# Rotating a 8192 x 8192 float32 matrix on one core: the first block of loads and the last one divided by rows

## The chip, the cores and the metric

The kernel runs on one core of one Trainium2 chip. The metric is device time in microseconds (us) of that core, from start to end of one execution; lower is better. The median of 19 runs stands for the kernel before.

## The reference

```
def setup_inputs():
    return {"x": np.random.randn(8192, 8192).astype(np.float32), "k": 1}

def reference(x, k):
    return np.rot90(x, k)
```

With k = 1 this is a quarter turn: `out[i, j] = x[j, 8191 - i]`, a transpose with the order of columns reversed. No arithmetic is done on the values. 268.44 MB have to be read and 268.44 MB written.

## The kernel before

The matrix is taken in 16 macro tiles: 8 bands of 1024 rows (`R`), and in each band two blocks of 4096 columns (`C`). A macro tile passes through these steps.

- Load (L82, issued by SP, the sync engine). Eight row tiles of 128 rows x 4096 columns, 2 MB each, one DMA per row tile, into a pool of two buffers (`a_pool`).
- Reverse (L89, VectorE). Each row tile is copied in eight chunks of 512 columns. The copy reverses the order inside each group of 128 columns. The chunks are kept in a pool of 68 buffers (`r_pool`); a macro tile needs 64 of them.
- Transpose (L104, TensorE). For each group of 128 columns the eight row tiles are transposed, 128 x 128 at a time, against an identity matrix, into PSUM. A PSUM tile holds 2048 values per partition, that is two groups of columns x 1024 rows, and needs 16 transposes. There are two PSUM tiles.
- Evict (L109, ScalarE). Each PSUM tile is copied to half of an output buffer. There are two output buffers (`o_pool`), each of 2 MB: four groups of columns x 1024 rows.
- Store (L115, issued by ScalarE's own queue). When two copies have filled a buffer, it is stored as one DMA of 2 MB: in each of the 128 partitions four pieces of 1024 values, 4 KB each, go to four rows of the output that lie 128 rows apart.

So a macro tile has eight loads and eight stores, all of 2 MB. No store of a macro tile can be made before its last load has landed, because each store needs all its row tiles.

`whole_reads` changes the source side of the stores alone: the four pieces of a partition, which lie side by side in the buffer, are described as one read of 16 KB.

What orders the work: loads stand in one queue on SP, stores in one queue on ScalarE, and a DMA that waits for a buffer holds the ones behind it in the same queue. VectorE, TensorE and ScalarE each run their instructions in a fixed order. Waits come from the pools: a load waits until VectorE has copied everything out of the buffer it takes, a copy of ScalarE waits until the store that last used its output buffer has landed. A scheduler sets the order of the instructions on each engine when the program is built, so it can differ from the order of the loops in the source. In the kernel before, the order of loads and stores is that of the loops.

Of the kernel before, what the change touches and what calls it, by code (L numbers as in the profile page):

```python
# [2 lines left out]

# [5 lines left out]

P = 128  # L10

R = 1024
RT = R // P
CH = 512
G = 4
PW = 2


def whole_reads(nc):

    for fn in nc.m.functions:
        for block in fn.blocks:  # L30
            for n, ins in enumerate(block.instructions):
                if not isinstance(ins, mybir.InstDMACopy):
                    continue
                src = ins.ins[0]
                ap = [list(d) for d in src.ap]
                if len(ap) == 3 and ap[2][0] == 1 and ap[1][0] == ap[2][1]:
                    ap = [ap[0], [1, 1], [1, ap[1][1] * ap[2][1]]]
                    block.instructions[n] = copy.replace(
                        ins,
                        ins=[copy.replace(src, ap=ap)],  # L40
                        ant_dge_precooked=False,
                    )


def widths(first, last, M):

    return [M // 2] * 2


@with_exitstack  # L50
def kernel(
    ctx: ExitStack,
    tc: tile.TileContext,
    x: bass.AP,
    k: bass.AP,
    out: bass.AP,
):
    nc = tc.nc
    assert k == 1, f"only k=1 supported, got {k}"
    nc.at_finalize(whole_reads)  # L60

    N, M = x.shape
    dt = x.dtype

    consts = ctx.enter_context(tc.tile_pool(name="consts", bufs=1))
    ident = consts.tile([P, P], dt)
    make_identity(nc, ident)

    a_pool = ctx.enter_context(tc.tile_pool(name="a_pool", bufs=2))
    r_pool = ctx.enter_context(tc.tile_pool(name="r_pool", bufs=68))  # L70
    o_pool = ctx.enter_context(tc.tile_pool(name="o_pool", bufs=2))
    psum_pool = ctx.enter_context(
        tc.tile_pool(name="psum", bufs=2, space=bass.MemoryType.PSUM)
    )

    for r0 in range(0, N, R):
        c0 = 0
        for C in widths(r0 == 0, r0 + R == N, M):
            chunks = {}
            for t in range(RT):  # L80
                a = a_pool.tile([P, C], dt, tag="a")
                nc.sync.dma_start(  # L82
                    out=a[:], in_=x[r0 + t * P : r0 + (t + 1) * P, c0 : c0 + C]
                )


                for j in range(C // CH):
                    ar = r_pool.tile([P, CH // P, P], dt, tag="ar")
                    nc.vector.tensor_copy(  # L89
                        out=ar[:],  # L90
                        in_=a[:, j * CH : (j + 1) * CH].rearrange(
                            "r (b m) -> r b m", m=P
                        )[:, :, ::-1],
                    )
                    chunks[t, j] = ar

            for g0 in range(0, C // P, G):
                o = o_pool.tile([P, G, R], dt, tag="o")
                for h in range(0, G, PW):
                    ps = psum_pool.tile([P, PW, R], mybir.dt.float32)  # L100
                    for w in range(PW):
                        g = g0 + h + w
                        for t in range(RT):
                            nc.tensor.transpose(  # L104
                                ps[:, PW - 1 - w, t * P : (t + 1) * P],
                                chunks[t, g * P // CH][:, g % (CH // P), :],
                                ident,
                            )
                    nc.scalar.copy(o[:, G - PW - h : G - h, :], ps[:])  # L109

                top = M - c0 - (g0 + G) * P
                dst = out[top : top + G * P, r0 : r0 + R].rearrange(
                    "(g m) f -> m g f", g=G
                )
                nc.scalar.dma_start(out=dst, in_=o[:])  # L115
            c0 += C


# [1 line left out]
_INS = ['x', 'k']  # L120
_OUTS = [((8192, 8192), 'float32')]

_NUMBERS = {'k': 1}


# [26 lines left out]
```

## Time and profile before

| what | value |
|---|---|
| median of 19 runs | 1280.13 us |
| lowest and highest run | 1276.9 and 1281.83 us |
| the profiled execution's own time | 1281.83 us |
| its span, first to last instruction | 1280.0 us |
| bytes moved by DMA | 537.55 MB, mean 420 GB/s |
| TensorE matmul, busy | 725.6 us (57%) |
| ScalarE, busy | 467.0 us (36%), 256 copies of 1871 ns |
| VectorE, busy | 354.9 us (28%), 1024 copies of 420 ns |
| loads | 128 of 2 MB, median 16.7 us from issue to landing |
| stores | 128 of 2 MB, median 15.9 us from issue to landing |

How to read the profile: the page gives the busy time of each engine, then the span cut in 40 equal slices with the busy share of each engine in tenths (9 is 90% or more), and under them the share and the rate of the 16 DMA engines. The chain is followed back from the last instruction: at each step to what released it. The timeline lists instructions in the order of time: start, duration, engine, line, operation, tiles, count, and in brackets the idle time before and what ended it. SPq and ACTq are the queues of SP and of ScalarE, with DMA issues among others; a duration there is no transfer time. DMA shares can come out a little over 1. A row of windows has the stretch and its length, the busy time and count of PE, PEld, DVE (VectorE), ACT (ScalarE) and POOL, the granted TensorE clock, the DMA share, and GB/s.

### The profile page before, as it was taken

The numbers are of one execution on the slowest core, as the hardware profiler recorded it, in microseconds if no ns is written. First come the engines' busy times: TensorE is split into PE (matmuls) and PEld (weight loads), VectorE is DVE, ScalarE is ACT, GpSimd is POOL, SyncE is SP. The second block draws the span as 40 slices with busy tenths as digits, with TensorE's granted clock in tenths as the row PEclk, the third lists the DMA queues.
The fourth block names the chain that finished last, engine by engine and source line by source line (L and its number), as shares of the span: only waits on it lengthen the run. The fifth ranks groups of instructions, "written<-read, shape, count | busy, mean of one in ns | idle before, by whom it ended". The sixth has DMA issues, their size and how long they took to land.

```text
span 1280.0 us, 10385 instructions
## 1 busy us (share of the span) xinstructions
PE 725.6 (57%) x4096; PEld 691.6 (54%) x4096; DVE 354.9 (28%) x1024; ACT 467.0 (36%) x257; POOL 0.7 (0%) x6
## 2 busy tenths in 40 slices
PE   0446655655556556565555665656556655656574
PEld 0345555654555556555555664655556645555464
DVE  3423222322322232223222322232223222322210
ACT  0233334333433343343334333433343334333455
POOL 0000000000000000000000000000000000000000
PEclk9967767677786776868777677686776686776878
DMA  9999999999999999999999999999999999999988
GB/s 352 347 428 430 426 430 423 424 428 429 428 430 429 426 426 424 427 430 429 429 428 430 429 424 428 428 426 424 429 428 428 422 425 424 426 427 427 428 363 358
DMA packets 36913, 537.55 MB, mean 420 GB/s; under 512 B 4096, under 2 KB 4096, under 8 KB 4096
## 3 DMA queue, kind: packets, MB, share of 16 engines
q10 hardware_dynamic: 18432, 268.44, 49.7%
q1 hardware_dynamic: 18432, 268.44, 49.6%
q8 instruction: 32, 0.52, 0.2%
q14 instruction: 17, 0.14, 0.0%
HBM read 268.44 MB, written 268.44 MB: 419 GB/s over the span
## 4 chain that ended last, share of the span: by engine, by line
DMA 79%; ACT 18%; DVE 1%; issue 1%; PE 0%; ACTq 0%; SPq 0%
DMA out_dram<-o 76%; ACT o L109 18%; DMA a<-in_x_dram 3%; DVE ar L89 1%; PE ps L104 0%; ACTq L109 0%; ACTq L115 0%; SPq L82 0%
## 5 line engine op out<-in xcount | busy, mean ns | idle before, releaser
L104 PE MATMUL ps<-ident,ar 128*128 128x128 f32 x4096 | 725.6, 360 | 542.8 <-ACT o L109 496.2
L104 PEld LDWEIGHTS ps<-ident,ar 128*128 128x128 f32 x4096 | 691.6, 193 | 576.6 <-ACT o L109 526.5
L109 ACT COPY o<-ps 128x2048 f32<-128x2048 f32 x256 | 465.7, 1871 | 804.8 <-DMA out_dram<-o 752.5
L89 DVE COPY ar<-a 128x512 f32<-128x512 f32 x1024 | 354.9, 420 | 873.6 <-DMA a<-in_x_dram 873.6
L109 ACT ACT_TABLE_LOAD x1 | 1.3, 1283 | 0.7 <-PEq L133 0.7
masks.py:199 POOL TENSOR_SCALAR_AFFINE_SELECT ident<-ident 128x128 f32<-128x128 f32 x1 | 0.3, 295 | 0.1
masks.py:197 POOL MEMSET ident<- 128x128 f32 x1 | 0.2, 205 | 0.3 <-POOLq L133 0.3
L133 POOL MEMSET const-bfloat16-1.0<- 128x1 bf16 x1 | 0.1, 103 | 0.0
L133 POOL MEMSET const-uint8-127<- 128x1 uint8 x1 | 0.1, 103 | 0.0
L133 POOL MEMSET const-float32-0.0<- 128x1 f32 x1 | 0.1, 100 | 0.2 <-issue 0.2
L133 POOL MEMSET const-float32-1.0<- 128x1 f32 x1 | 0.1, 100 | 0.0
## 6 DMA issues: line engine op xcount, KB each, us to landing
a<-in_x_dram SPq DMA_DIRECT2D x128, 2048.0 KB, 16.7
out_dram<-o ACTq DMA_DIRECT2D x128, 2048.0 KB, 15.9
```

Source lines behind the costliest of these rows:

```text
L89: nc.vector.tensor_copy(out=ar[:], in_=a[:, j * CH : (j + 1) * CH].rearrange("r (b m) -> r b m", m=P)[:, :, ::-1],)
L104: nc.tensor.transpose(ps[:, PW - 1 - w, t * P : (t + 1) * P], chunks[t, g * P // CH][:, g % (CH // P), :], ident,)
L109: nc.scalar.copy(o[:, G - PW - h : G - h, :], ps[:])
L133: nc = _bacc.Bacc("TRN2", target_bir_lowering=False, num_devices=1)
```

## The change

A generator, `macro_tiles`, now yields the blocks. All are of 4096 columns. The first macro tile is divided by rows into blocks of 256, 256 and 512 rows, the last one into two of 512 rows; the other 14 stay at 1024. PSUM tiles and output buffers keep their size, so a block with fewer rows puts more groups of columns into each: with 256 rows a store has 16 pieces of 1 KB in each partition, with 512 rows eight pieces of 2 KB. Every store stays at 2 MB, but for the last, which goes out in two of 1 MB. The counts of loads, transposes and copies stay the same.

The third and fourth loads of the loop (`loads in (2, 3)`) take their buffers from `o_pool`. In the last block the first two output buffers are taken from `a_pool`.

In the new kernel loads are at L102, VectorE's copies at L109, transposes at L130, ScalarE's copies at L135 and stores at L143.

```diff
-R = 1024
-RT = R // P
+RT = 8
+W = 4096
 CH = 512
-G = 4
-PW = 2
+E = 4096
+PB = 2048
...
+def macro_tiles(N, M):
+    for r0 in range(0, N, RT * P):
+        for c0 in range(0, M, W):
+            rows = [RT]
+            if r0 == 0 and c0 == 0:
+                rows = [2, 2, 4]
+            if r0 + RT * P == N and c0 + W == M:
+                rows = [4, 4]
+            r = r0
+            for n in rows:
+                yield r, n, c0
+                r += n * P
...
+    tiles = list(macro_tiles(N, M))
+    loads = 0
+    for r0, rt, c0 in tiles:
+        last = (r0, rt, c0) == tiles[-1]
+        R = rt * P
+        G = E // R
+        PW = PB // R
+        chunks = {}
+        for t in range(rt):
+            if loads in (2, 3):
+                a = o_pool.tile([P, E], dt, tag="o")
+            else:
+                a = a_pool.tile([P, W], dt, tag="a")
+            loads += 1
+            nc.sync.dma_start(
+                out=a[:], in_=x[r0 + t * P : r0 + (t + 1) * P, c0 : c0 + W]
+            )
...
+        for g0 in range(0, W // P, G):
+            if last and g0 < 2 * G:
+                ot = a_pool.tile([P, E], dt, tag="a")
+            else:
+                ot = o_pool.tile([P, E], dt, tag="o")
+            o = ot.rearrange("m (g f) -> m g f", g=G)
+            S = PW if last and g0 + G == W // P else G
+            for h in range(0, G, PW):
+                ps = psum_pool.tile([P, PW, R], mybir.dt.float32)
...
+                nc.scalar.copy(o[:, G - PW - h : G - h, :], ps[:])
+                done = h + PW
+                if done % S == 0:
+                    top = M - c0 - (g0 + done) * P
+                    dst = out[top : top + S * P, r0 : r0 + R].rearrange(
+                        "(g m) f -> m g f", g=S
+                    )
+                    nc.scalar.dma_start(
+                        out=dst, in_=o[:, G - done : G - done + S, :]
+                    )
```

More of the change, by code (lines that the diff above doesn't have):

```diff
@@ L42, in whole_reads @@
                     )
-def widths(first, last, M):
-    return [M // 2] * 2
+def macro_tiles(N, M):
[10 more added lines that the diff above has]
+                r += n * P
 @with_exitstack
@@ L74 @@
     )
[L76 to L83, printed above, removed]
-                )
[L87 to L93, printed above, removed]
-                    )
[L95 to L116, printed above, removed]
@@ new lines @@
+    tiles = list(macro_tiles(N, M))
[15 more added lines that the diff above has]
+            )
+            for j in range(W // CH):
+                ar = r_pool.tile([P, CH // P, P], dt, tag="ar")
+                nc.vector.tensor_copy(
+                    out=ar[:],
+                    in_=a[:, j * CH : (j + 1) * CH].rearrange(
+                        "r (b m) -> r b m", m=P
+                    )[:, :, ::-1],
+                )
+                chunks[t, j] = ar
+        for g0 in range(0, W // P, G):
[7 more added lines that the diff above has]
+                ps = psum_pool.tile([P, PW, R], mybir.dt.float32)
+                for w in range(PW):
+                    g = g0 + h + w
+                    for t in range(rt):
+                        nc.tensor.transpose(
+                            ps[:, PW - 1 - w, t * P : (t + 1) * P],
+                            chunks[t, g * P // CH][:, g % (CH // P), :],
+                            ident,
+                        )
[5 more added lines that the diff above has]
+                        "(g m) f -> m g f", g=S
+                    )
+                    nc.scalar.dma_start(
+                        out=dst, in_=o[:, G - done : G - done + S, :]
+                    )
```

## The prediction

> **What bounds the kernel now.** I read the page's table of slices first, then the chain of work that ended last, then the four stages by windows, then the timeline at both ends. Times are us from the span's start; load n and store n count the 2 MB transfers (2.097 MB each) from 0 to 127 in the order of the loops.
>
> ```profile
> DMA  9999999999999999999999999999999999999988
> GB/s 352 347 428 430 426 430 423 424 428 429 428 430 429 426 426 424 427 430 429 429 428 430 429 424 428 428 426 424 429 428 428 422 425 424 426 427 427 428 363 358
> ...
> DMA 79%; ACT 18%; DVE 1%; issue 1%; PE 0%; ACTq 0%; SPq 0%
> ```
>
> The DMA engines are busy in every slice and carry the chain (79%). But four slices, two at each end, move 350 to 360 GB/s where the others move about 427. A kernel with fixed bytes can only win or lose there. The windows put edges on it: the first store is issued at 57.40, store 8 at 136.32, and store 119 at 1226.95, just after the last load landed (1225.75).
>
> ```profile
> 0.74:57.40 56.66, 10.80 (x48) 7.54 (x48) 23.34 (x68) 5.01 (x3) 0.49 (x2) 1.00 0.92 350
> 57.40:136.32 78.92, 44.75 (x250) 42.80 (x249) 22.19 (x65) 29.10 (x16) 0.00 (x0) 0.71 1.00 425
> 136.32:1226.95 1090.63, 638.00 (x3554) 611.31 (x3553) 307.80 (x889) 403.79 (x222) 0.00 (x0) 0.74 1.01 427
> 1226.95:1280.00 53.05, 32.03 (x250) 29.90 (x248) 1.57 (x5) 29.08 (x16) 0.00 (x0) 0.85 0.85 357
> ```
>
> The last three columns are granted clock, DMA share and GB/s. Read-only ramp: 350 GB/s at a share of 0.92. Write-only tail: 357 at 0.85. In between, 16 transfers take 78.92 us, 4.9 us each.
>
> ```profile
> 8.00 2.77 DVE L89 COPY ar<-a 128x512 f32<-128x512 f32 x8 [8.00 <-DMA a<-in_x_dram]
> ...
> 12.88 2.77 DVE L89 COPY ar<-a 128x512 f32<-128x512 f32 x8 [2.11 <-DMA a<-in_x_dram]
> ...
> 50.88 2.77 DVE L89 COPY ar<-a 128x512 f32<-128x512 f32 x8 [4.52 <-DMA a<-in_x_dram]
> ...
> 51.36 8.03 PE L104 MATMUL ps<-ident,ar 128*128 128x128 f32 x50 [6.60 <-DVE ar L89]
> 53.58 3.79 ACT L109 COPY o<-ps 128x2048 f32<-128x2048 f32 x2 [51.56 <-PE ps L104]
> ...
> 57.40 0.64 ACTq L115 DMA_DIRECT2D out_dram<-o  x1
> ...
> 61.75 0.56 ACTq L115 DMA_DIRECT2D out_dram<-o  x1
> ```
>
> In the ramp each load waits for a copy to free one of two buffers; loads 0, 1 and 7 land at 8.00, 12.88 and 50.88, so from load 1 on a load takes (50.88-12.88)/6, about 6.3 us. From load 7 to the first store 6.5 us pass, to the second 4.35 more.
>
> ```profile
> 1251.66 3.64 ACT L109 COPY o<-ps 128x2048 f32<-128x2048 f32 x2 [1.26 <-DMA out_dram<-o]
> ...
> 1255.33 0.55 ACTq L115 DMA_DIRECT2D out_dram<-o  x1
> 1257.22 3.63 ACT L109 COPY o<-ps 128x2048 f32<-128x2048 f32 x2 [1.92 <-DMA out_dram<-o]
> ...
> 1272.57 0.55 ACTq L115 DMA_DIRECT2D out_dram<-o  x1
> ```
>
> In the tail ScalarE waits for an output buffer before each pair of copies: store n+2 follows the landing of store n. Issues lie some 5.6 us apart, where 4.9 would be the DMA's own pace, and a store lands 7.4 us after its issue (1272.57 to 1280.0).
>
> **What the skill says.** "DMA: Bandwidth & Descriptors", section Anatomy of one DMA, gives (for the GpSimd path) 2.0 us plus bytes/436e3: an estimate of 6.8 us for these 2.097 MB; the trace has 7.26 (0.74 to 8.00) and 7.4, which I use. The same section says that a semaphore wait happens on the issuing sequencer before dispatch. So a load that waits on SP holds all loads behind it; nothing in the trace of before separates the two, as its loads stand in the order of need. Its section Why small descriptors are slow prices a packet at 3 cycles beyond its 32-byte beats. No row before has pieces under 4 KB on the store side.
>
> **The change, start.** The diff says that the third and fourth loads go to idle output buffers. Read against the loop they don't: block one (256 rows) takes loads 0 and 1, and its stores 0 and 1 take both output buffers before loads 2 and 3 ask for them. The built program's instruction order confirms it. SP issues loads 0, 1, 4, 5, 2, 3, 6, 7; load 2 waits for store 0 to land and load 3 for store 1. VectorE copies 0, 1, 2, 3, 4, 5 in this order, so 4 and 5, already landed, lie behind 2 and 3, and load 6, which needs the buffer of 4, waits too.
>
> Prices: 1.5 us from issue to first data and 1.0 from last data to landing (my split of 7.4-4.9); 4.9 us a transfer, twice that for each of two queues that share; 5.5 for a load alone (350/0.92 = 380 GB/s). Matmuls after a pause cost 0.234 us (13 in 3.04, from 51.36 on), then 0.158 (28 in 4.43).
>
> 1. Loads 0 and 1 land at 8.0 and 12.9 as before; loads 4 and 5 take the freed buffers and land at 19.0 and about 27 (25.6 before, now shared with store 0).
> 2. Store 0: copies reach the first transpose at 13.36; a PSUM tile of 16 transposes needs 15 more, at 0.234 us, and the second tile 16: 19.25. Two ScalarE copies of 1.87: issue at 21.1, 8.2 after load 1. Store 1: 25.5.
> 3. Store 0 has data from 22.6, shares with load 5 until 26.2, ends 29.3, lands 30.3. Load 2 is issued then. Store 1 ends 36.6, lands 37.6; load 3 is issued. Load 2 lands 40.4, load 3 behind it in the queue at 45.9.
> 4. VectorE: load 3 until 48.7, then 4 until 51.5 and 5 until 54.2. Load 6 is issued at 51.5, load 7 at 54.2, store 2 at 45.9+8.2 = 54.1, store 3 at 58.5. Between 44.9 (data of load 3) and 53.0 (data of load 6) no transfer exists: 8.1 us of empty DMA.
> 5. Loads 6, 7 and stores 2, 3 share: load 7 lands 71.6. Block three (512 rows): store 4 issued 7.5 later, 79.1, data 80.6. Loads 8 and 0.45 of 9 are done by then.
> 6. Stores 4 to 7 beside loads: four times 9.8, to 119.8; loads reach 0.45 of load 13. Loads 14, 15 and the rest of 13 run alone, since no store can be made before load 15 closes the next block: 2.55 times 6.2 (15.8). Landing 136.6; store 8 at +6.5: 143.1.
>
> Before, store 8 went out at 136.32, and store 0 at 57.40 with load 8 landed, the same state as now at store 8: from there both kernels run the same. Ramp: 143.1-136.3 = +6.8 us. Early stores help the first 57 us, but the empty 8 us and a second read-only stretch take more.
>
> **The change, end.** Bytes after the last load are the same nine stores. The first five keep the two-buffer chain (store 123 issued near 1250.4, landing 1257.2). Stores 124 and 125 go to the load buffers, free since the last VectorE copy: ScalarE runs on at 2 times 1.9 to 1.95, issues at 1254.2 and 1258.1, then 126 at 1262 (its buffer, store 122's, landed 1251.6) and the halves of 127 at 1263.9 and 1265.9. Now data follows data: from 1256.2 four times 4.9 = 1275.8, landing 1276.8 instead of 1280.0: -3.2. TensorE hides behind ScalarE as long as a tile of 16 transposes takes 1.9 (32 in 3.74 in most rows of the tail); at the 2.7 that one row has (32 in 5.38), store 126 goes out at 1266 and the gain shrinks to 1.7. One store issue more on ACT (0.55) lies in the slack of 0.5 to 5.5 us by which data of earlier stores hold these back. That the first half of the last block is loaded complete four loads earlier brings nothing: its stores 120 to 123 wait for buffers of stores in flight.
>
> **Smaller pieces.** Four stores in 1 KB pieces and twelve in 2 KB pieces. By the skill's packet price, my estimate: 35 beats a KB, 140 per 4 KB, against 131, 6.9% or 0.34 us each, and 0.11 for 2 KB. On the path lie all of them at most: 4x0.34+12x0.11 = 2.7. Below: 0, since extra packets may hide between two queues; a gain is excluded, as no byte is saved. I take 1.3. If the engine paid per piece far more, see the rivals.
>
> **Sum.** 6.8-3.2+1.3 = +4.9. On the profiled execution (1281.83, span 1280.0) that gives 1286.7; it lies 1.7 over the median of the runs, 1280.13, so the forecast for the median is 1285.
>
> **Rivals.**
> Balance: steps 3 to 6 are 2 to 6 us too long (transfers overlapping better, store 0 earlier by fewer cold matmuls). For it: load 1 landed 4.88 after load 0, reading alone at full pace. Against: five later loads took 6.3. Net within 2.6 us: about 1280.
> Faster: the early ramp runs at its shortest latencies. Store 0 at 19.4 (6.5 after load 1), landing 26.8; load 2 at 34.2, load 3 at 39.1; store 2 at 45.6; load 7 at 66.5; store 4 at 73; stores 4 to 7 to 113.7; 2.4 loads at 5 us: store 8 at 133.5, -2.8. With the tail -3.2 and no price for pieces: 1274. It decides only if store 8 is issued before 136.9; by 139.5 the two ends cancel. Against it: the read-only rows of before.
> Dear pieces: a 1 KB piece at half speed adds 4.9 to each of stores 0 to 3, nearly all on the path: about 1300. The trace can't exclude it.
> The change not doing what it says (no idle buffer is used early) is part of the forecast, not a rival.
>
> **Chances.** Forecast (net +2.6 to +11) 0.60; dear pieces 0.10; balance 0.20; faster 0.10. About 0.2% is what a measurement of this kernel can tell from no change. So faster 0.10, same 0.20, slower 0.70. The range takes forecast and balance, with the pieces' 0 to 2.7 and the ramp's +4 to +9: 1278 to 1291; the outer two cases, 0.20, are left out.
>
> **What would show it.** Right: load 2 issued at the landing of store 0 (28 to 31), a hole in the DMA near 45 to 53, store 2 near 54, store 8 near 143 (below 136.9 the forecast is wrong), a read-only stretch before it, and a tail whose last four stores are queued, ending some 23 us after store 124. A store 0 that takes over 11 us from issue to landing, or a 2 KB store of the tail over 7.7, shows dear pieces.

## The result and the profile after

The changed kernel takes 1295.68 us (median of 7 runs, 1291.61 to 1296.67) against 1280.09 us before (median of 45): 15.6 us slower, ratio 1.0118, 95% interval 1.0107 to 1.0128. The profiled execution took 1293.74 us with a span of 1291.9 us, 11.9 us more than the span before. The forecast was 1285 with a range of 1278 to 1291: the direction held, the size did not.

The page of the changed kernel, the same three rows as before:

```profile
DMA  9799999999999999999999999999999999999988
GB/s 367 248 374 425 377 427 429 429 429 426 427 428 428 429 429 428 428 427 425 427 429 430 429 428 429 429 429 428 428 427 427 428 430 430 428 430 428 422 370 358
...
DMA 78%; ACT 18%; DVE 1%; issue 1%; PE 1%; ACTq 0%; SPq 0%; DVEq 0%
```

Each slice is 32 us. The second one fell to 248 GB/s (347 before), the third and fifth to 374 and 377 (428 and 426 before). The middle is unchanged, and the last two slices are as slow as they were. So the loss lies in the first 160 us, and the new end gained nothing that the slices show. The windows of the changed kernel (the last two columns are DMA share and GB/s):

```profile
21.39:30.00 8.61, 1.97 (x16) 1.73 (x16) 0.00 (x0) 3.63 (x2) 0.00 (x0) 0.74 1.01 379
30.00:36.00 6.00, 0.00 (x0) 0.00 (x0) 0.00 (x0) 0.00 (x0) 0.00 (x0) 0.50 1.04 248
...
49.16:57.00 7.84, 7.03 (x48) 6.75 (x49) 7.84 (x24) 3.65 (x2) 0.00 (x0) 0.76 0.20 49
...
65.00:77.50 12.50, 1.11 (x4) 0.71 (x4) 2.84 (x9) 0.00 (x0) 0.00 (x0) 0.50 1.01 370
...
122.00:150.18 28.18, 8.92 (x44) 7.22 (x44) 11.09 (x32) 3.73 (x2) 0.00 (x0) 0.53 0.96 380
150.18:1239.06 1088.88, 647.69 (x3546) 615.93 (x3545) 308.42 (x890) 403.55 (x222) 0.00 (x0) 0.73 1.01 427
1239.06:1263.00 23.94, 18.63 (x142) 17.56 (x141) 2.14 (x7) 14.54 (x8) 0.00 (x0) 0.89 0.85 357
1263.00:1291.90 28.90, 12.68 (x110) 11.61 (x108) 0.00 (x0) 14.54 (x8) 0.00 (x0) 0.82 0.88 363
```

Two kinds of loss stand side by side. From 49.16 to 57.00 the engines have almost nothing to move: share 0.20. From 30 to 36, and from 65 to 77.5, they are wholly busy, share 1.04 and 1.01, and yet move 248 and 370 GB/s where a full share meant 425 to 427 before. A share of 1 is not a rate.

The timeline gives the dates that the forecast had named, here loads 2 and 3 landing (VectorE's first copy), and stores 2, 4 and 8:

```profile
43.65 2.77 DVE L109 COPY ar<-a 128x512 f32<-128x512 f32 x8 [28.04 <-DMA a<-in_x_dram]
...
49.16 8.14 DVE L109 COPY ar<-a 128x512 f32<-128x512 f32 x24 [2.74 <-DMA a<-in_x_dram]
...
56.78 0.55 ACTq L143 DMA_DIRECT2D out_dram<-ot  x1
...
85.66 0.55 ACTq L143 DMA_DIRECT2D out_dram<-ot  x1
...
150.18 0.55 ACTq L143 DMA_DIRECT2D out_dram<-ot  x1
```

The waits of SP's queue in the first 60 us confirm the wait for stores, a row that the kernel before has not:

```profile
SPq L102 <- DMA out_dram<-ot: 23.3, 2, 14.3
```

The row gives the total, the count and the longest: two loads waited 23.3 us in all, 14.3 at most. The 24 copies in one piece from 49.16 are loads 3, 4 and 5: 4 and 5 had landed long before and stood behind. Store 8 went out at 150.18, 13.9 later than before and 7.1 later than forecast.

### The profile page after: what moved, and what is told of

Read it like the earlier page. It is cut to its first block, busy times and chain, and to the rows that moved or that the text cites. A ratio compares the mean times of both kernels' runs of the same rounds, so it can differ in the third digit from the quotient of the medians.

```text
span 1291.9 us, 10410 instructions
## 1 busy us (share of the span) xinstructions
PE 731.3 (57%) x4096; PEld 691.3 (54%) x4096; DVE 354.7 (27%) x1024; ACT 466.9 (36%) x257; POOL 0.7 (0%) x6
## 4 chain that ended last, share of the span: by engine, by line
DMA 78%; ACT 18%; DVE 1%; issue 1%; PE 1%; ACTq 0%; SPq 0%; DVEq 0%
DMA out_dram<-ot 70%; ACT ot L135 18%; DMA a<-in_x_dram 7%; DVE ar L109 1%; PE ps L130 1%; ACTq L143 0%; ACTq L135 0%; SPq L102 0%; DVEq L109 0%
## 5 line engine op out<-in xcount | busy, mean ns | idle before, releaser
L130 PE MATMUL ps<-ident,ar 128*128 128x128 f32 x4096 | 731.3, 361 | 546.2 <-ACT ot L135 453.2
L130 PEld LDWEIGHTS ps<-ident,ar 128*128 128x128 f32 x4096 | 691.3, 193 | 585.9 <-ACT ot L135 483.6
L135 ACT COPY ot<-ps 128x2048 f32<-128x2048 f32 x256 | 465.7, 1870 | 812.0 <-DMA out_dram<-ot 697.8
L109 DVE COPY ar<-a 128x512 f32<-128x512 f32 x1024 | 354.7, 420 | 886.5 <-DMA a<-in_x_dram 886.5
```

Of the source, the lines that this page charges most:

```text
L109: nc.vector.tensor_copy(out=ar[:], in_=a[:, j * CH : (j + 1) * CH].rearrange("r (b m) -> r b m", m=P)[:, :, ::-1],)
L130: nc.tensor.transpose(ps[:, PW - 1 - w, t * P : (t + 1) * P], chunks[t, g * P // CH][:, g % (CH // P), :], ident,)
```

## The experiments

Theory after the result: two causes at the start, the wait for stores with the order it leads to, and pieces of 1 KB that cost far more than the packet price; and an end that is worth nothing. Rivals: the wait alone did all of it; or the pieces alone; or the new end gains its 3 us and the start costs 3 more.

**Start and end apart.** Two kernels, each with one end of the change.

```diff
 e1: -                rows = [4, 4]
     +                rows = [RT]
     -            if last and g0 < 2 * G:
     +            if False:
     -            S = PW if last and g0 + G == W // P else G
     +            S = G
 e2: -                rows = [2, 2, 4]
     +                rows = [RT]
     -            if loads in (2, 3):
     +            if False:
```

> The divided first tile with its two loads in output buffers, and the last tile and its buffers as before the change. Theory (the loss is all at the start, the new end is worth nothing): about 1295, as the full change. Rival (the end does gain the 3.2 us of the forecast, and the start costs more): about 1298 to 1299. If the end does harm: below 1294.

> First tile whole and all loads in the load buffers as before; only the last tile is divided and uses load buffers for two stores. Theory: 1280, no change, because a store alone in the queue moves at about 403 GB/s, 5.2 us, so that queued stores cannot follow each other every 4.9 us. Rival, the forecast: 1277. If 2 KB pieces are dear: 1282 or more.

The start alone took 1293.1 us beside 1279.62 before (ratio 1.0111, 1.0094 to 1.0128), the end alone 1279.61 (1.0001, 0.9991 to 1.0011). So the loss is at the start, and the forecast's -3.2 is refuted. e1 lies below 1294, where its expectation had put an end that does harm; but its interval overlaps that of the full change, and e2, with 14 runs, shows no harm. The traces agree: from the issue of store 119 to the end pass 52.3 to 53.7 us in the seven with the new end (the change, e2, e3, e4, e7, e8, e9) and 52.5 to 53.8 us in the three with the old one (the kernel before, e1, e11).

**Without the wait.** All loads in load buffers, pieces of 1 KB kept.

```diff
-            if loads in (2, 3):
+            if False:
```

> The change, but loads 2 and 3 use load buffers: no load waits for a store any more, and loads are issued in the order 0, 1, 2, 3, 4, while the 1 KB pieces of the first four stores stay. If the wait and the order it leads to are the main cost: 1281 to 1285. If small pieces are the main cost (about 7 of the 14 us): 1287 to 1289. If the wait costs nothing: 1295.

1286.16 us (1.0047, 1.0032 to 1.0062): 6.5 slower than before. Taking the wait away saves 9.5 us, and the result falls between the two ranges of the expectation: the wait alone does not explain the loss.

**The price of a piece, by itself.** The kernel before, with all 128 stores cut into smaller pieces (here 1 KB, Q = 4; 2 KB is Q = 2). The pieces go to other places of the output, so what it holds is not the rotated matrix; the bytes and the number of stores stay.

```diff
-                top = M - c0 - (g0 + G) * P
-                dst = out[top : top + G * P, r0 : r0 + R].rearrange(
-                    "(g m) f -> m g f", g=G
-                )
-                nc.scalar.dma_start(out=dst, in_=o[:])
+                i = g0 // G
+                top = M - c0 - C + (i // Q) * Q * G * P
+                c = r0 + (i % Q) * (R // Q)
+                dst = out[top : top + Q * G * P, c : c + R // Q].rearrange(
+                    "(g m) f -> m g f", g=Q * G
+                )
+                src = o.rearrange("m g (q f) -> m (g q) f", q=Q)
+                nc.scalar.dma_start(out=dst, in_=src)
```

> The kernel before, with every store cut into 16 pieces of 1 KB per partition; pieces go to other places of the output than the reference's, the bytes are the same. If the four 1 KB stores of the change cost some 1.6 us each by their pieces: 128 of them cost 200, about 1480. If the packet price of the forecast holds (0.34 us each): 1324. If pieces cost nothing beside loads: 1280.

> The same with 8 pieces of 2 KB per partition, again to other places. Packet price of the forecast, 0.11 us each: 1294. Nothing: 1280. Dear (half of what 1 KB costs): 1380.

With 1 KB pieces 1485.7 us beside 1280.65 (1.1517, 1.1425 to 1.161): 205 us on 128 stores, 1.60 us each (1.43 to 1.61 by the interval; the four runs lie between 1465.18 and 1487.76). With 2 KB 1291.91 (1.0083, 1.0056 to 1.011): 11.3 us, 0.09 each. Their middle stretches, 1 KB first, then 2 KB, then the kernel before:

```profile
200.00:1400.00 1200.00, 591.85 (x3348) 561.49 (x3349) 288.58 (x832) 381.42 (x210) 0.00 (x0) 0.72 1.01 365
```

```profile
200.00:1200.00 1000.00, 575.17 (x3228) 551.21 (x3227) 280.30 (x808) 367.48 (x202) 0.00 (x0) 0.75 1.01 424
```

```profile
200.00:1200.00 1000.00, 585.42 (x3256) 561.11 (x3257) 282.81 (x816) 371.05 (x204) 0.00 (x0) 0.74 1.01 427
```

The share is 1.01 in all three; 365, 424 and 427 GB/s. Halving the pieces once costs almost nothing, halving them again costs some 1.5 us a store. The price does not need loads beside the stores: after the last load the stores leave 6.8 us apart in e5 (1435.02 to 1475.83, six steps), 5.7 in the kernel before (1238.21 to 1272.57). The 1.6 of the expectation came from the trace of the changed kernel: store 4 left at 85.66, 6.6 us after its forecast date, with four stores of 1 KB pieces ahead of it.

**Wait and pieces, crossed.** The full change with its first eight stores written in 4 KB pieces, again to other places of the output, with the wait (e7) and without it (e8).

```diff
+                    src = o[:, G - done : G - done + S, :]
+                    if stores < 8:
+                        top = M - W + 512 * stores
+                        dst = out[top : top + 512, 0:1024].rearrange(
+                            "(g m) f -> m g f", g=4
+                        )
+                        src = ot.rearrange("m (g f) -> m g f", g=4)
+                    stores += 1
 e8: -            if loads in (2, 3):
     +            if False:
```

> The full change, but the first eight stores write 4 KB pieces (to other places of the same region of the output than the reference's); waits, order and bytes stay. If the 1 KB pieces cost 1.6 us each and the wait and order the rest: 1287 to 1289. If the pieces' cost was hidden beside the wait: 1294 or more. If the pieces are all of it: 1281.

> The same 4 KB pieces, and loads 2 and 3 in load buffers, so that no load waits for a store. If pieces and wait are the two causes and nothing else: 1279 to 1281, as before the change. If dividing the first tile costs by itself (a second read-only stretch): 1283 or more. If early stores help: 1277.

e7 took 1286.37 us beside 1279.93 (1.005, 1.0038 to 1.0061), e8 1279.34 (0.9992, 0.9985 to 0.9999). Medians of the four corners (from several sessions, in which the kernel before stayed between 1279.6 and 1280.1):

| | 1 KB and 2 KB pieces | 4 KB pieces |
|---|---|---|
| loads 2, 3 wait for stores | 1295.68 | 1286.37 |
| no load waits for a store | 1286.16 | 1279.34 |

Either cause alone costs some 7 us; together they cost 16.3. The 2.5 us by which this exceeds the sum of both are not clear of the noise: e1, whose start is that of the change, took 1293.1, and sent store 8 at 147.46 in its trace where the changed kernel has 150.18. The trace shows where the two causes meet: load 3 waits for store 1, and store 1 is what the pieces slow. Between the issue of load 2 and that of load 3, first in the changed kernel, then in e7:

```profile
30.35:39.68 9.33, 0.00 (x0) 0.00 (x0) 0.00 (x0) 0.00 (x0) 0.00 (x0) 0.50 1.01 288
```

```profile
30.93:36.39 5.46, 0.00 (x0) 0.00 (x0) 0.00 (x0) 0.00 (x0) 0.00 (x0) 0.50 1.00 420
```

9.33 us at 288 GB/s against 5.46 at 420, with the same two transfers in flight. Dividing the first tile, with neither cause, costs nothing: 1279.34 is 0.6 below the kernel before.

**What the edit could have been.** The first tile whole (e3), or in two halves (e9): then no store holds an output buffer yet when loads 2 and 3 ask for one.

```diff
 e3: -                rows = [2, 2, 4]
     +                rows = [RT]
 e9: -                rows = [2, 2, 4]
     +                rows = [4, 4]
```

> The change, but the first tile stays whole (1024 rows), so that its loads 2 and 3 really find idle output buffers: the four first loads are issued at once. Theory: the first four loads follow each other every 4.9 to 5.5 us instead of 6.3, 2 to 4 us gained at the start: 1276 to 1278. Rival (reads alone are slow whatever the number of buffers): 1280.

> The change, with the first tile in two blocks of 512 rows instead of 256, 256 and 512: the first block then has four loads, so that loads 2 and 3 are asked for before any store holds an output buffer, and pieces are 2 KB. Theory (the DMA is kept full from the start either way, early stores add nothing): about as with the whole first tile, 1273 to 1275. If early stores pay: 1268 to 1271. If the divided tile costs: 1278 or more.

e3: 1273.2 us beside 1279.62 (0.9949, 0.9935 to 0.9963). e9: 1275.55 beside 1279.93 (0.9968, 0.9956 to 0.998). Both beat the kernel before, and e3 by more than its expectation had said. Its timeline shows why:

```profile
8.13 2.77 DVE L109 COPY ar<-a 128x512 f32<-128x512 f32 x8 [8.13 <-DMA a<-in_x_dram]
...
13.02 2.77 DVE L109 COPY ar<-a 128x512 f32<-128x512 f32 x8 [2.12 <-DMA a<-in_x_dram]
...
27.69 2.77 DVE L109 COPY ar<-a 128x512 f32<-128x512 f32 x8 [2.12 <-DMA a<-in_x_dram]
...
32.59 2.77 DVE L109 COPY ar<-a 128x512 f32<-128x512 f32 x8 [2.12 <-DMA a<-in_x_dram]
...
50.10 0.65 ACTq L143 DMA_DIRECT2D out_dram<-ot  x1
```

Six loads land 4.9 us apart, the pace of the full DMA, with nothing but reads in flight. Store 0 goes out at 50.10 instead of 57.40. Reading alone is not slow in itself; two buffers were too few to keep it supplied. In e9 store 0 goes out at 30.67, some 20 us earlier than in e3, and yet e9 is no faster: it is 2.4 us slower, with intervals that overlap a little, and 0.5 above the range expected if early stores add nothing. So early stores don't pay here.

**The start alone, and a better end.** e11 is the kernel before with loads 2 and 3 in output buffers and nothing else. e10, and once more as e12 on the chip of e11, adds an end in which the last eight stores take two load buffers and two output buffers in turn, in 4 KB pieces.

```diff
 e11: e3, and the end as in e1
 e10: e3, and
      -                rows = [4, 4]
      +                rows = [RT]
      -            if last and g0 < 2 * G:
      +            if last and g0 // G % 4 < 2:
```

> First tile whole with loads 2 and 3 in output buffers; last tile whole too, its stores taking two load buffers and two output buffers in turn, the last store in two halves. A store alone moves in 5.2 us, and the two-buffer chain of the last stores issues every 5.6: eight stores then gain 2 to 3 us, 1270 to 1271. If the end is bound by the DMA queue alone: 1273, as with the whole first tile.

> The kernel before with one thing added: the third and fourth load take the two idle output buffers; both ends of the matrix stay whole, the last stores use two buffers as before. Theory: all of the gain of the whole first tile is this, about 1273. If the divided end had a part in it: 1275 or more.

> The four-buffer end once more, on the same chip as the kernel with the start alone. If issuing the last stores without waiting is worth something: 2 to 3 us less than that kernel. If the DMA queue bounds the end alone: the same within 1 us.

e11: 1273.38 us beside 1280.86 (0.9946, 0.9933 to 0.9958). e10: 1270.71 beside 1279.93 (0.9927, 0.9914 to 0.9939); e12: 1271.18 beside 1280.86 (0.992, 0.9907 to 0.9934). The gain of e3 is all in the two loads. The better end adds about 2.2 us on the same chip; as the intervals of e11 and e12 just touch, its size is less certain than its sign. From the issue of store 119 to the end, the traces of e10 and e12 take 50.6 and 50.1 us, that of e11 52.5. This end differs from that of the change in two things, the number of stores that need not wait and the size of the pieces; which of them brings the gain was not tried apart. e10 is the fastest version found, 9 us under the kernel before.

## Why the prediction was wrong

The wait for stores came as forecast. Two terms of the sum failed: the smaller pieces, put at 1.3, measured 6.7 to 9.3, and the end, put at -3.2, measured 0.

**The wait and the order (steps 1 to 6, +6.8): right.** e7 runs them with 4 KB pieces, and its dates follow the forecast. Load 2, load 3, store 2, load 6, load 7, store 4 and store 8 in e7:

```profile
40.64 2.78 DVE L110 COPY ar<-a 128x512 f32<-128x512 f32 x8 [24.96 <-DMA a<-in_x_dram]
45.89 8.14 DVE L110 COPY ar<-a 128x512 f32<-128x512 f32 x24 [2.47 <-DMA a<-in_x_dram]
...
53.90 0.55 ACTq L152 DMA_DIRECT2D out_dram<-ot  x1
...
60.40 2.78 DVE L110 COPY ar<-a 128x512 f32<-128x512 f32 x8 [6.37 <-DMA a<-in_x_dram]
70.18 2.77 DVE L110 COPY ar<-a 128x512 f32<-128x512 f32 x8 [7.00 <-DMA a<-in_x_dram]
...
77.56 0.55 ACTq L152 DMA_DIRECT2D out_dram<-ot  x1
...
141.13 0.55 ACTq L152 DMA_DIRECT2D out_dram<-ot  x1
```

Forecast: 40.4, 45.9, 54.1, 61.8 (load 6, worked out with the forecast's rates), 71.6, 79.1 and 143.1. The first three are met within 0.3 us; from load 6 on e7 is 1.4 to 2.0 us early. The hole was forecast at 44.9 to 53.0; in e7 at most 8 GB/s move from 45 to 52, in the changed kernel at most 16 from 48 to 55.5.

The 6.8 counts the whole new start, with pieces at no cost, against the kernel before. By medians that is 6.4 (e7 less the kernel before). In the traces store 8 leaves 4.8 us later (141.13 against 136.32), and the two profiled executions differ by 4.5. So the mechanism held, and that the medians come so close to 6.8 is in part luck. The wait with its order, alone, is 7.0 (e7 less e8). How much of these 7 us belongs to VectorE's order and how much to the wait on SP was not tried apart.

**The smaller pieces (+1.3): the step that failed.** The forecast took half of 2.7, an estimate from the packet price in the Trainium skill, "DMA: Bandwidth & Descriptors", section Why small descriptors are slow: 0.34 us for a store in 1 KB pieces, 0.11 for one in 2 KB pieces. For 2 KB the measurement agrees, 0.09 (e6). For 1 KB it is 1.60 (e5; at least 1.43), more than four times the estimate, and the measurement decides. So the term is 4 times 1.6 = 6.4 and a little for 2 KB. It measured 6.8 without the wait (e4 less e8), and with it 6.7 (e1 less e7) to 9.3 (the change less e7); whether the wait makes it dearer stays open. The prediction also named the rival, dear pieces, with a chance of 0.10 and about 1300 us. Its price of 4.9 was three times too high, but its sign for it, a store 0 of more than 11 us, did not show: store 0 landed 9.0 us after its issue (21.39 to 30.35). The sign was on the wrong store. Store 1, beside load 2, took 13.9 (25.73 to 39.61); the forecast had 12.1. The second sign named for dear pieces, a 2 KB store of the tail over 7.7, could not decide: the kernel before has one of 7.95 with 4 KB pieces (1260.88 to 1268.83). The estimate took a piece for a packet; the profile counts 36913 packets in the kernel before, in e5 and in e6 alike, so its packets are not the pieces. Why 1 KB costs so much more than 2 KB the runs don't tell.

**The end (-3.2): wrong, measured 0.** The issues came nearly as forecast: store 124 left 27.7 us after store 119 (forecast 27.3), the last half 40.6 us after it (forecast 39.0; the whole store 45.6 before). What failed is the step after them, that four queued stores follow each other every 4.9 us and land 1.0 us after their last data. The last windows of the changed kernel:

```profile
1263.00:1270.00 7.00, 5.85 (x52) 5.34 (x51) 0.00 (x0) 6.19 (x4) 0.00 (x0) 1.00 0.96 400
1270.00:1277.00 7.00, 6.42 (x59) 6.11 (x58) 0.00 (x0) 5.65 (x4) 0.00 (x0) 1.00 0.98 393
1277.00:1284.00 7.00, 0.41 (x4) 0.17 (x2) 0.00 (x0) 2.70 (x2) 0.00 (x0) 0.84 1.00 418
...
1289.00:1290.00 1.00, 0.00 (x0) 0.00 (x0) 0.00 (x0) 0.00 (x0) 0.00 (x0) 0.50 0.08 33
1290.00:1291.00 1.00, 0.00 (x0) 0.00 (x0) 0.00 (x0) 0.00 (x0) 0.00 (x0) 0.50 0.02 8
```

and of the kernel before:

```profile
1277.00:1278.00 1.00, 0.00 (x0) 0.00 (x0) 0.00 (x0) 0.00 (x0) 0.00 (x0) 0.50 0.66 279
1278.00:1279.00 1.00, 0.00 (x0) 0.00 (x0) 0.00 (x0) 0.00 (x0) 0.00 (x0) 0.50 0.62 262
1279.00:1280.00 1.00, 0.00 (x0) 0.00 (x0) 0.00 (x0) 0.00 (x0) 0.00 (x0) 0.50 0.00 0
```

Queued stores moved (400+393+418)/3 = 404 GB/s, 5.2 us each: 4 times 0.3 is 1.2. From the end of the bulk at 1289 a trickle of 33 and 8 GB/s runs to 1291, and the landing is at 1291.9: 2.9 us, where the kernel before has 1.0 after data that end at 279 and 262 GB/s. The 1.2 and the 1.9 make 3.1, about the whole forecast gain. This is the account of one trace; in e2, with the same end, the rate was 414 GB/s (1256 to 1273). That one engine of sixteen lags after several queued stores, and holds the last landing, would fit the 33 GB/s (418/16 is 26), but this is argued, not shown.

**A lone load takes 5.5 us: wrong, with little weight.** e3 has 4.9, and the error lies within the 2.0 us by which store 8 comes early in e7. The 380 GB/s had been read from a stretch in which only two buffers supplied the queue. So the forecast also missed what idle buffers are worth when the loads really get them, 7.5 us by e11.

**The sum.** Forecast 6.8+1.3-3.2 = 4.9. By medians: dividing with neither cause -0.6 (e8 less the kernel before), the wait 7.0, the pieces beside the wait 9.3, together 15.7. These steps lead from the kernel before to the changed one, so they meet the measured 15.6 by construction, and it is no further check; the new end is in all of these kernels but the first, and e2 puts it at 0.

## What to carry to other kernels

A price that has not been measured at the size in question can fail by more than its own bound: cut the whole kernel's transfers to the new size once, and divide. Before a transfer is put into an idle buffer, follow the loop to the line that asks for that buffer first, and see what stands behind the waiting transfer. Where a stretch has one kind of transfer only, ask whether its rate is that of the engines or that of too few buffers.

## What the runs showed of the hardware

- A store of 2 MB costs 0.09 us more in 2 KB pieces than in 4 KB, and 1.4 to 1.6 us more in 1 KB pieces (e6, e5). The DMA share stays at 1.01, so the loss can't be seen in the share, only in GB/s. The pieces lie in rows of the output that are 128 rows apart; other layouts were not tried.
- Reads alone reach the pace of the mixed stretch, a 2 MB transfer every 4.9 us (e3), with two more buffers for loads 2 and 3.
- Stores alone with several queued moved 404 GB/s in 2 KB pieces (the change) and 420 in 4 KB pieces (e10, 1226 to 1264), where the mixed stretch has 427. After the bulk come some 2 us under 50 GB/s: 33 and 8 in the change, 49 and 16 in e10.
